# Three modulation vectors of the first layer on TensorE in column tiles instead of on VectorE

## The chip, the cores and the metric

The kernel runs on one core of one Trainium2 chip. A core has a matrix engine (TensorE, "PE" in the profile, with its weight loads as "PEld"), a vector engine (VectorE, "DVE"), a scalar engine (ScalarE, "ACT"), GpSimd ("POOL") and SyncE ("SP"), which here issues the transfers from memory. Each engine works through its own list of instructions in order and waits on semaphores for the others. The metric is the device time of one execution in microseconds (us), lower is better. The kernel before takes 1732.04 us (median of 3 runs, 1729.26 to 1732.41).

## The reference

A two-layer backbone over 512 latent tokens and 256 context tokens, width 1024, in float32. Each layer first computes six modulation vectors for the latent stream (from `c`) and six for the context (from `c_ctx`):

```python
mod   = (jax.nn.silu(c)     @ w_mod[l] + b_mod[l]).reshape(b_, 6, 1, d)
mod_c = (jax.nn.silu(c_ctx) @ w_mod[l] + b_mod[l]).reshape(6, d)
sh1, sc1, g1, sh2, sc2, g2 = [mod[:, i] for i in range(6)]
z = modulate(x, norm1_g, sh1, sc1) @ w_in          # modulate: rms_norm(x) * (1 + scale) + shift
...                                                # gMLP (A), neighbourhood attention (B), mLSTM (C)
x = x + g1 * (concat([y_a, y_b, y_c]) @ w_out)
x = x + g2 * swiglu(modulate(x, norm2_g, sh2, sc2), w_gate, w_up, w_down)
```

The change concerns vectors 2, 3 and 4 of layer 0: `g1` (the mixing gate), `sh2` and `sc2` (shift and scale of the second norm), for both streams. Each is a product of a 1024-vector with a 1024 x 1024 matrix, so 3 x 4 MB of weights for two vectors each. They are first needed after the mixing sub-layer, when the output projection's result is added to `x`.

## The kernel before

Activations are kept transposed: 128 features on the partitions, tokens along the free axis. Every float32 weight block (128 x 1024, 512 KB) is loaded into a buffer of the pool `wraw` (three buffers), split into a rounded high part `whi` on ScalarE (L128) and a rest `wlo` on VectorE (L129), each in a pool of three, and multiplied as high x high, high x low and low x high (`dense`, L152, results in `dps`). One block gives 24 products for the latents (512 columns) and 24 for the context (256 columns).

The first layer runs as follows. Vectors 0 and 1 are computed on TensorE at the start (`mod_first`, L180 to L195): the two silu'd condition vectors stand in `c_act`, padded with zeros to 32 columns for each of 8 feature blocks; a product with `c_act` as the stationary operand therefore uses a 128 x 32 column tile of the array, and four feature blocks go to the four column tiles. The 32-row partial results in PSUM (`modps`) are copied to `modsb` by ScalarE and summed over the four tiles by a small product with a selection matrix `csum` (L188).

Then comes the mixing stage, about 60 to 410 us. `ORDERS[0]` is a string that interleaves pieces of work: `B0` to `B2` attention over pairs of heads, `C0` to `C2` mLSTM, `A`, `v`, `r`, `o`, and `m`, one step of the modulation. A scheduler of the framework then sets the order of each engine's list from that program; the list is what runs. In `B`, one attention unit (`attend`) is: scores on TensorE (`bsps`, L539), bias, maximum, exponential and normalising on VectorE and ScalarE (L559 to L566, `prob`), transposition on TensorE (`ptps`, L569), copy on ScalarE (L571), product with the values (`bops`, L539). Each head pair has six units in layer 0 (three inner, one edge, two context) and four in layer 1, which has no context output.

A modulation step before (`mod_steps`, L206 to L221) is one of 24 for vectors 2, 3 and 4: a load of a 512 KB block `wmod` into a `wraw` buffer (L209), and two VectorE instructions over 128 x 1024 elements that multiply with a condition row and accumulate (L212, one for each stream). After eight steps a bias add (L217). The same function serves vector 5 and all of layer 1, later, beside the feed-forward part; that is not changed.

The output projection (`lagged`) follows at about 407 us, uses `g1` in `resid` (L1076), and its context products use the PSUM pool `md`, which has one bank.

Of the kernel before, what the change touches and what calls it, by code (L numbers as in the profile page):

```python
# [9 lines left out]
F32 = mybir.dt.float32  # L10
F32R = mybir.dt.float32r
AF = mybir.ActivationFunctionType
ALU = mybir.AluOpType
# [4 lines left out]
D = 1024  # L18
KD = 8
# [24 lines left out]
def tile_backbone(ctx: ExitStack, tc: tile.TileContext, A, out):  # L44
    nc = tc.nc
    te, ve, ac, gp, sp = nc.tensor, nc.vector, nc.scalar, nc.gpsimd, nc.sync

    const = ctx.enter_context(tc.tile_pool(name="const", bufs=1))
    par = ctx.enter_context(tc.tile_pool(name="par", bufs=1))
    hyp = ctx.enter_context(tc.tile_pool(name="hy", bufs=1))  # L50
    wraw = ctx.enter_context(tc.tile_pool(name="wraw", bufs=3))
# [15 lines left out]
    csum = cst[:, C_SUM:C_SUM + 2]  # L67
# [36 lines left out]
    def zat(name, dt=F32):  # L104
        return za.tile([128, 768], dt, tag="z", name=name)
# [97 lines left out]
    def mod_steps(l, vs):  # L203
# [20 lines left out]

        return [lambda v=v, i=i: step(v, i) for v, i in items]

    def load_small(l):
        t = par.tile([128, NSMALL], F32, tag="small%d" % l, name="small")
        link(sp.dma_start(out=t, in_=A["small"][l]))
        o, v = 0, {}  # L230
        for n, w in (("bmod", 48), ("n1", 8), ("n2", 8), ("cw", 18), ("cb", 6), ("gb", 24), ("fg", 8)):
            v[n] = t[:, o:o + w]
            o += w
        return v
# [66 lines left out]
    def x_tiles():  # L301
        return [(zat if k < 7 else zct)("x%d" % k) for k in range(KD)]

    c_act = zat("c_act")[:, 0:KD * 32].rearrange("p (k s) -> p k s", k=KD)
    gp.memset(c_act, 0.0)
    xd = drp.tile([KD, 128, 768], F32, name="xd")

# [6 lines left out]
    for toks in ((2, 3, 4, 5), (0, 1)):  # L314
        raws = []
# [127 lines left out]
    for l in range(2):  # L443
# [6 lines left out]
        latc = [P_lat] if last else [P_lat, P_ctx]  # L450
        lat_off = [(256, NL)] if last else [(256, NL), (0, NC)]
        fill_rate[0] = FILL_MIX
        mixmods = [] if last else mod_steps(0, (2, 3, 4))

        def do_mods():
            for f in mixmods:
# [768 lines left out]
def layout(inputs):  # L1225
# [14 lines left out]
    def blocks(w):  # L1240
        return w.reshape(L, w.shape[1] // 128, 128, w.shape[2] // 128, 128).transpose(0, 3, 2, 1, 4).reshape(
            L, w.shape[2] // 128, 128, w.shape[1])

    def ksplit(w, nk):
# [2 lines left out]

    wi, wg, wu, wd = I["w_in"], I["w_gate"], I["w_up"], I["w_down"]
    wm = I["w_mod"].reshape(L, D, 6, 8, 128).transpose(0, 2, 3, 4, 1)
    wm0 = I["w_mod"][0].reshape(8, 128, 6, 8, 128)[:, :, 0:2].transpose(3, 1, 0, 2, 4).reshape(8, 128, 2048)  # L1250
    arr = {
        "x": I["x"][0], "ctx": I["ctx"][0], "cond": cond, "cond_rows": np.broadcast_to(np.stack([I["c"][0], I["c_ctx"]]), (128, 2, D)), "w_mod": wm, "w_mod0": wm0, "win_blk": blocks(wi[:, :, 0:3200]),
        "win_wave": ksplit(np.concatenate([wi[:, :, 896:1024], wi[:, :, 1280:1408], wi[:, :, 512:640]], axis=2), 2),
        "win_cv": ksplit(np.concatenate([wi[:, :, 2432:2816], wi[:, :, 3200:3224]], axis=2), 2),
        "win_av": ksplit(wi[:, :, 256:512], 4), "w_out": blocks(I["w_out"]), "w_gate": blocks(wg), "w_up": blocks(wu),
# [23 lines left out]
```

## Time and profile before

| what | value |
|---|---|
| median of 3 runs | 1732.04 us |
| the profiled execution: its own time | 1729.28 us |
| its span in the profile, mean granted TensorE clock | 1726.4 us, 0.984 |
| ScalarE busy, GpSimd busy (share of the span) | 615.3 us (36%), 148.2 us (9%) |
| data moved | 184.11 MB, mean 107 GB/s |
| mixing stage of layer 0 | about 60 to 410 us |
| same stage of layer 1 | about 1050 to 1310 us |

The difference of 2.9 us between the profiled execution's time and its span lies around the traced instructions. In a group's row stand: line, engine, operation, written tile <- read tiles, shape, count | busy us, mean ns of one | idle time of the engine just before these instructions and what ended it. A product of two float32 operands has two records in the trace, so eight such products show as x16. In a row of windows stand, behind the stretch and its length, the busy us of each engine with the number of records, the granted clock, and the transfers' share and rate.

### The profile page before, as it was taken

To read this page: it belongs to the slowest core of one execution; us is meant where nothing else is said; L and a number is where in the kernel's file an instruction comes from. 1 tells how busy PE (TensorE), PEld (TensorE's weight loads), DVE (VectorE), ACT (ScalarE), POOL (GpSimd) and SP (SyncE) were. 2 spreads that over 40 slices of the span, in tenths; PEclk is the share of its full clock that TensorE was granted. 3 is DMA by queue.
4 is the path that set the end of the run, shared out by engine and by line. 5 is a ranking of instruction groups with operands and counts; after the bars stand their busy time and mean duration, and the time that the engine had idled before them with its cause. 6 is when DMAs were issued, how large, how long until landed. Compare 5 with 4: busy or idle time off the path is not lost.

```text
span 1726.4 us, 26247 instructions
## 1 busy us (share of the span) xinstructions
PE 1660.5 (96%) x10784; PEld 1416.0 (82%) x10784; DVE 936.3 (54%) x1697; ACT 615.3 (36%) x1126; POOL 148.2 (9%) x157
## 2 busy tenths in 40 slices
PE   7998999889999999999999999989989999999998
PEld 5886777768888888888888889777869988888888
DVE  4589787635475555344443355585675633333335
ACT  4444344633332211222112244534654522222225
POOL 0000112122200000000000020012033000000000
PEclk9999999979999999999999999989999999999999
DMA  8742313213244434334333233210213322222222
GB/s 290 250 151 70 123 59 102 74 35 102 62 136 132 123 122 135 125 126 128 122 122 104 74 117 105 71 56 28 86 62 117 105 98 98 93 94 94 98 82 95
DMA packets 57143, 184.11 MB, mean 107 GB/s; under 512 B 6720, under 2 KB 8384, under 8 KB 56896
## 3 DMA queue, kind: packets, MB, share of 16 engines
q1 hardware_dynamic: 57024, 182.45, 32.7%
q8 instruction: 84, 1.38, 0.3%
q14 instruction: 35, 0.29, 0.1%
HBM read 175.08 MB, written 7.34 MB: 106 GB/s over the span
## 4 chain that ended last, share of the span: by engine, by line
PE 69%; DVE 5%; ACT 2%; POOL 1%; issue 1%; DVEq 0%; ACTq 0%; POOLq 0%
PE dps L152 60%; PE wps L402 4%; PE vps L627 2%; PE ptps L569 1%; PE nps L876 1%; DVE wlo L129 1%; PE bops L539 1%; ACT pu L862 1%; DVE nm L561 0%; ACT prob L564 0%; DVE prob L566 0%; ACT whi L128 0%; PE bsps L539 0%; DVE bsps L559 0%; PE ups L832 0%
## 5 line engine op out<-in xcount | busy, mean ns | idle before, releaser
L128 ACT ACTIVATE whi<-wraw 128x1024 fp32r<-128x1024 f32 (+2 forms) x224 | 226.6, 1013 | 694.8 <-PE dps L152 429.7
L129 DVE TENSOR_TENSOR wlo<-wraw,whi 128x1024 fp32r<-128x1024 f32 (+2 forms) x224 | 262.5, 1173 | 170.7 <-ACT whi L128 167.9
L152 PE MATMUL dps<-h2lh,wlo 128*128 128x512 f32 (+1 forms) x664 | 258.3, 391 | 0.0
L152 PE MATMUL dps<-h2ll,whi 128*128 128x512 f32 (+1 forms) x664 | 258.3, 391 | 0.0
L152 PE MATMUL dps<-h2lh,whi 128*128 128x512 f32 (+1 forms) x664 | 257.6, 389 | 0.0
L152 PE MATMUL dps<-gh,whi 128*128 128x512 f32 (+1 forms) x576 | 175.2, 341 | 0.0
L152 PE MATMUL dps<-gl,whi 128*128 128x512 f32 (+1 forms) x576 | 175.2, 340 | 0.0
L152 PE MATMUL dps<-gh,wlo 128*128 128x512 f32 (+1 forms) x576 | 175.1, 340 | 0.0
L212 DVE SCALAR_TENSOR_TENSOR wmod<-wmod,c_all 128x1024 f32<-128x1024 f32 x80 | 98.5, 1231 | 98.5 <-DMA wmod<-in_w_mod 97.7
L152 PEld LDWEIGHTS dps<-h2lh,whi 128*128 128x128 f32 x664 | 124.3, 188 | 27.7
L152 PEld LDWEIGHTS dps<-h2lh,wlo 128*128 128x128 f32 x664 | 124.2, 188 | 27.4
L152 PEld LDWEIGHTS dps<-h2ll,whi 128*128 128x128 f32 x664 | 124.3, 188 | 26.7
L1076 DVE SCALAR_TENSOR_TENSOR x<-dps,modT,x 128x512 f32<-128x512 f32 (+1 forms) x112 | 65.3, 596 | 138.0 <-PE dps L152 137.7
L152 PE MATMUL dps<-ll,whi 128*128 128x512 f32 x336 | 136.6, 407 | 1.2 <-DVE ll L109 1.2
L152 PE MATMUL dps<-lh,whi 128*128 128x512 f32 x336 | 134.8, 402 | 1.1 <-ACT whi L128 1.1
L152 PE MATMUL dps<-lh,wlo 128*128 128x512 f32 x336 | 134.7, 401 | 0.0
L152 PEld LDWEIGHTS dps<-gl,whi 128*128 128x128 f32 x576 | 99.3, 188 | 13.5 <-DVE gl L109 0.2
L152 PEld LDWEIGHTS dps<-gh,whi 128*128 128x128 f32 x576 | 99.3, 188 | 13.2
L152 PEld LDWEIGHTS dps<-gh,wlo 128*128 128x128 f32 x576 | 99.3, 188 | 13.2
L212 DVE SCALAR_TENSOR_TENSOR junk<-wmod,c_all 128x1024 f32<-128x1024 f32 x48 | 58.9, 1227 | 76.8 <-DMA wmod<-in_w_mod 76.8
L1153 DVE TENSOR_TENSOR silu<-silu,dps 128x512 f32<-128x512 f32 (+1 forms) x64 | 37.4, 589 | 107.4 <-PE dps L152 107.4
L152 PE MATMUL dps<-h2cl,whi 128*128 128x256 f32 x328 | 92.5, 282 | 0.0
(320 smaller groups left out, 3123.2 us busy)
## 6 DMA issues: line engine op xcount, KB each, us to landing
wmod<-in_w_mod SPq DMA_DIRECT2D x80, 512.0 KB, 3.6
wraw<-in_w_up SPq DMA_DIRECT2D x42, 512.0 KB, 3.2
wraw<-in_w_gate SPq DMA_DIRECT2D x40, 512.0 KB, 3.2
wraw<-in_win_blk SPq DMA_DIRECT2D x34, 512.0 KB, 3.7
wraw<-in_w_down SPq DMA_DIRECT2D x32, 512.0 KB, 3.2
wraw<-in_w_out SPq DMA_DIRECT2D x19, 512.0 KB, 3.3
wraw<-in_w_down SPq DMA_DIRECT2D x21, 384.0 KB, 3.1
wraw<-in_win_cv SPq DMA_DIRECT2D x16, 408.0 KB, 3.2
```

The source lines that it names most:

```text
L128: ac.activation(out=hi[:, 0:n], in_=raw[:, 0:n], func=AF.Copy)
L129: ve.tensor_tensor(out=lo[:, 0:n], in0=raw[:, 0:n], in1=hi[:, 0:n].bitcast(F32), op=ALU.subtract)
L152: m = te.matmul(out=ps[:, 0:T], lhsT=wt[:, c], rhs=(flo if wh else fhi)(k), start=(k == 0 and wi == 0), stop=(k == nk - 1 and wi == 2),)
L212: ve.scalar_tensor_tensor(out=junk if t < nt - 1 else raw, in0=raw, scalar=1.0, in1=c_all[:, t, :], op0=ALU.mult, op1=ALU.mult, accum_out= ...
L402: m = te.matmul(out=ps[:, 0:T], lhsT=wt[:, cs_], rhs=(flo if wh else fhi)(k), start=(k == 0 and wi == 0), stop=(k == KD - 1 and wi == 2))
L539: m = te.matmul(*args, **kw)
L569: te.transpose(out=tps[:, i * 128:(i + 1) * 128], in_=pt[:, i * 128:(i + 1) * 128], identity=ident)
L627: te.matmul(out=vps[i][:, 0:408], lhsT=tokslice(nm, k, i), rhs=wt[:, cs], start=(k == 0 and wi == 0), stop=(k == KD - 1 and wi == 2))
L862: tabled.append(ac.activation(out=tc_, in_=pc, func=AF.Exp, scale=-1.0, bias=g_))
L876: m = te.matmul(out=banks[j][64 * hf:64 * hf + 64, c * 65:(c + 1) * 65], lhsT=lhsT, rhs=rhs, start=start, stop=stop, skip_group_check=True)
L1076: ve.scalar_tensor_tensor(out=xs, in0=ps, scalar=modT[:, row * 8 + k, g[3]:g[3] + 1], in1=xs, op0=ALU.mult, op1=ALU.add)
L1153: ve.tensor_tensor(out=s, in0=s, in1=pui, op=ALU.mult)
```

## The change

`mod_steps(0, (2, 3, 4))` in the mixing stage is replaced by `mod_pe_steps()`. There are again 24 steps, one for a vector v and a block i of 128 outputs. Step n loads the block of step n + 1 (the first step loads its own too) into a `wraw` buffer and multiplies the block it holds with `c_act`: eight products of 128 columns into one of the four quarters of a PSUM bank of the pool `md`. After every fourth step ScalarE copies the bank to `modsb` (128 x 512), four small products with `csum` sum the column tiles, and VectorE adds the bias for four blocks at once. So `c_act` has to live on: it moves from a `za` buffer to the constants. The weights come in another layout (`w_modp`), with the same bytes. `ORDERS` is the same.

```diff
+    def mod_pe_steps():
+        modT, sm = mods[0], smalls[0]
+        items = [(v, i) for v in (2, 3, 4) for i in range(KD)]
+        raws, bank = {}, [None]
+
+        def load(n):
+            if n < len(items):
+                v, i = items[n]
+                raws[n] = wraw.tile([128, D], F32, tag="w", name="wmod")
+                sp.dma_start(out=raws[n], in_=A["w_modp"][v - 2, i])
+
+        def step(n):
+            v, i = items[n]
+            if n == 0:
+                load(0)
+            load(n + 1)
+            raw = raws.pop(n)
+            q = i % 4
+            if q == 0:
+                bank[0] = pst(md, "modps")
+            ps = bank[0]
+            for kp in range(KD):
+                te.matmul(
+                    out=ps[32 * (kp % 4):32 * (kp % 4) + 32, q * 128:(q + 1) * 128], lhsT=c_act[:, kp, :],
+                    rhs=raw[:, kp * 128:(kp + 1) * 128], start=(kp < 4), stop=(kp >= 4), tile_position=(0, 32 * (kp % 4)))
+            if q < 3:
+                return
+            sb = wkt("modsb")
+            ac.activation(out=sb, in_=ps, func=AF.Copy)
+            for c in range(4):
+                te.matmul(out=ps[:, 2 * c:2 * c + 2], lhsT=sb[:, c * 128:(c + 1) * 128], rhs=csum)
+            r = v * 8 + i - 3
+            ve.tensor_tensor(
+                out=modT[:, r:r + 4, :], in0=ps[:, 0:8].rearrange("p (c t) -> p c t", c=4),
+                in1=sm["bmod"][:, r:r + 4].unsqueeze(2).to_broadcast([128, 4, 2]), op=ALU.add)
+            if v == 4 and i == KD - 1:
+                ve.scalar_tensor_tensor(
+                    out=a2s[0], in0=modT[:, 32:40, :], scalar=1.0, in1=sm["n2"].unsqueeze(2).to_broadcast([128, 8, 2]),
+                    op0=ALU.add, op1=ALU.mult)
+
+        return [lambda n=n: step(n) for n in range(len(items))]
...
-    c_act = zat("c_act")[:, 0:KD * 32].rearrange("p (k s) -> p k s", k=KD)
+    c_act = const.tile([128, KD * 32], F32, name="c_act").rearrange("p (k s) -> p k s", k=KD)
...
-        mixmods = [] if last else mod_steps(0, (2, 3, 4))
+        mixmods = [] if last else mod_pe_steps()
...
+    wmp = I["w_mod"][0].reshape(8, 128, 6, 8, 128)[:, :, 2:5].transpose(2, 3, 1, 0, 4).reshape(3, 8, 128, 1024)
```

Lines behind the new function stand 42 further on in the changed kernel: `ptps` is L569 before and L611 after, `bops` and `bsps` L539 and L581. The new products are L249, the small ones L257, the new loads L236.

The change moves instructions on all engines of the mixing stage. Three places matter. First SyncE's list, where the weights of `B1` (`win_blk`, the first three of them) stand among the loads of the modulation; the number behind a name tells one buffer's use from the next, and in brackets are the semaphores waited for. Before:

```order
L209 DMA wmod_1432<-in_w_mod 128x1024 [waits DMAHW4_49,DVE_49]
L209 DMA wmod_1561<-in_w_mod 128x1024 [waits DMAHW0_49,DVE_49]
L125 DMA wraw_1568<-in_win_blk 128x1024 [waits DMAHW1_49,DVE_49]
L125 DMA wraw_1628<-in_win_blk 128x1024 [waits DVE_49]
L125 DMA wraw_1688<-in_win_blk 128x1024 [waits DMAHW3_49,DVE_49]
```

Now:

```order
L236 DMA wmod_1424<-in_w_modp 128x1024 [waits DMAHW3_49,PE_49]
L236 DMA wmod_1453<-in_w_modp 128x1024 [waits DMAHW4_49,DMAHW0_49,PE_49]
L236 DMA wmod_1595<-in_w_modp 128x1024 [waits DMAHW6_49,DMAHW1_49,PE_49]
L125 DMA wraw_1609<-in_win_blk 128x1024 [waits DMAHW7_49,PE_49]
L569 DMA bias_1800<-in_bias 128x384 [waits DVE_49]
L569 DMA bias_1802<-in_bias 128x384 [waits DVE_49]
L125 DMA wraw_1669<-in_win_blk 128x1024 [waits DMAHW2_49,DVE_49,Activation_49]
```

The loads of the modulation, and the first weight load behind them, now wait for TensorE (`PE_49`), which has to have used the block that a buffer held; before they waited for VectorE alone.

Second, TensorE's list at the third inner unit of `B0`, from the transposition of its probabilities to the first dense products behind the edge unit's scores. Before:

```order
L569 MATMUL ptps<-cst,prob 128x128 x4
L152 MATMUL dps<-lh,wlo 128x512
L152 MATMUL dps<-ch,wlo 128x256
L152 MATMUL dps<-lh,whi 128x512
L152 MATMUL dps<-ch,whi 128x256
L539 MATMUL bops<-probT,bvt 64x128 x8
L539 MATMUL bsps<-bk,bq 64x128 x4
L539 MATMUL bsps<-bk,bq 128x256 x2
L152 MATMUL dps<-ll,whi 128x512
```

Now:

```order
L249 MATMUL modps<-wmod,c_act 32x128
L611 MATMUL ptps<-cst,prob 128x128 x4
L249 MATMUL modps<-wmod,c_act 32x128 x23
L611 MATMUL ptps<-cst,prob 128x128 x4
L581 MATMUL bops<-probT,bvt 64x128 x8
L581 MATMUL bsps<-bk,bq 64x128 x4
L581 MATMUL bsps<-bk,bq 128x256 x2
L152 MATMUL dps<-lh,whi 128x512
L152 MATMUL dps<-ch,whi 128x256
```

Three steps' products (24) stand in one bunch where dense products stood, and the dense products behind are the first of `B1`, with the weights `wraw_1609` of the list above, whose load waits for the last of these 24.

Third, TensorE's list at the first inner unit of `B1`, behind its scores `bsps`. Before:

```order
L478 MATMUL trps<-cst,bv 128x128 x4
L152 MATMUL dps<-lh,wlo 128x512
L539 MATMUL bsps<-bk,bq 128x256 x4
L152 MATMUL dps<-ch,whi 128x256
L152 MATMUL dps<-cl,whi 128x256
L152 MATMUL dps<-ch,wlo 128x256
```

Now:

```order
L520 MATMUL trps<-cst,bv 128x128 x6
L581 MATMUL bsps<-bk,bq 128x256 x4
L249 MATMUL modps<-wmod,c_act 32x128 x24
L611 MATMUL ptps<-cst,prob 128x128 x8
L152 MATMUL dps<-lh,whi 128x512
L152 MATMUL dps<-ch,whi 128x256
```

Before, 30 dense products stood between the scores and the first transposition; now it is 24 products of the modulation alone, and the dense products behind the transpositions start a new block, whose load waits for the middle eight of the 24.

More of the change, by code (lines that the diff above doesn't have):

```diff
@@ L1249, in layout @@
     wm = I["w_mod"].reshape(L, D, 6, 8, 128).transpose(0, 2, 3, 4, 1)
+    wmp = I["w_mod"][0].reshape(8, 128, 6, 8, 128)[:, :, 2:5].transpose(2, 3, 1, 0, 4).reshape(3, 8, 128, 1024)
     wm0 = I["w_mod"][0].reshape(8, 128, 6, 8, 128)[:, :, 0:2].transpose(3, 1, 0, 2, 4).reshape(8, 128, 2048)
     arr = {
-        "x": I["x"][0], "ctx": I["ctx"][0], "cond": cond, "cond_rows": np.broadcast_to(np.stack([I["c"][0], I["c_ctx"]]), (128, 2, D)), "w_mod": wm, "w_mod0": wm0, "win_blk": blocks(wi[:, :, 0:3200]),
+        "x": I["x"][0], "ctx": I["ctx"][0], "cond": cond, "cond_rows": np.broadcast_to(np.stack([I["c"][0], I["c_ctx"]]), (128, 2, D)), "w_mod": wm, "w_mod0": wm0, "w_modp": wmp, "win_blk": blocks(wi[:, :, 0:3200]),
         "win_wave": ksplit(np.concatenate([wi[:, :, 896:1024], wi[:, :, 1280:1408], wi[:, :, 512:640]], axis=2), 2),
```

## The prediction

> **What bounds the kernel now.** I read the page's busy times first, then the chain of work that ended last.
>
> ```profile
> span 1726.4 us, 26247 instructions
> PE 1660.5 (96%) x10784; PEld 1416.0 (82%) x10784; DVE 936.3 (54%) x1697; ACT 615.3 (36%) x1126; POOL 148.2 (9%) x157
> PE 69%; DVE 5%; ACT 2%; POOL 1%; issue 1%; DVEq 0%; ACTq 0%; POOLq 0%
> ```
>
> TensorE is busy for 96% of the span and carries 69% of the chain. Work added to it costs its own length unless it falls into an idle gap; work taken from VectorE gains only where TensorE waits for VectorE. So the question is how much TensorE idles, and for whom, in the stage that loses the VectorE work. The windows compare that stage with the same stage of layer 1, which has the same attention code and no modulation on VectorE:
>
> ```profile
> core 0: us, PE busy (x) PEld busy (x) DVE busy (x) ACT busy (x) POOL busy (x), PEclk, DMA share, GB/s
> 60.00:410.00 350.00, 316.76 (x2594) 263.12 (x2593) 253.39 (x542) 161.94 (x354) 54.89 (x54) 0.96 0.31 101
> 1050.00:1310.00 260.00, 243.34 (x1976) 201.67 (x1975) 165.77 (x366) 127.66 (x267) 46.45 (x52) 0.97 0.21 66
> ```
>
> In 60 to 410 us TensorE idles 350 - 316.8 = 33.2 us, and the clock that it is granted is 0.96, which is another 14 us of full speed. No gain in this stage can be above 47 us. In layer 1, idle is still 16.7 us of 260. The waits of TensorE, in 60 to 410 us (first three rows) and in 1050 to 1310 us (last row):
>
> ```profile
> PE ptps L569 <- DVE prob L566: 18.0, 12, 4.9
> PE sps L803 <- DVE rden L902: 2.1, 1, 2.1
> PE trps L478 <- DVE ck L772: 1.4, 1, 1.4
> ...
> PE ptps L569 <- DVE prob L566: 6.1, 10, 1.4
> ```
>
> More than half of the idle time is the softmax: the transposition waits until VectorE has normalised the probabilities.
>
> **What is removed.** The instructions at L212 in that stage, one row for each stream:
>
> ```profile
> L212 DVE SCALAR_TENSOR_TENSOR junk<-wmod,c_all x24: 1204/1222/1455, 84.1 to 309.6; 128x1024 f32<-128x1024 f32 x24
> L212 DVE SCALAR_TENSOR_TENSOR wmod<-wmod,c_all x24: 1202/1220/1896, 85.4 to 311.9; 128x1024 f32<-128x1024 f32 x24
> ```
>
> 48 instructions of 1.22 us are 58.6 us of VectorE's 253.4. VectorE is not the bound, so this is not a gain by itself. Where an L212 stands between two steps of a softmax, it delays `prob` by 1.2 us. Layer 1 shows what is left without them: 6.1 us in 12 attention units (three head pairs, four units each). Layer 0 has 18 units, so 6.1 x 18 / 12 = 9.2 us would stay, and 18.0 - 9.2 = 8.8 us go. Of the other two waits, 3.5 us, I take 2.2. **Term 1: -11 us.** Bounds: 0, since the new order also puts less work under some softmaxes (below), and -21.5, all three waits gone.
>
> **The clock.** The loss is concentrated late in the stage:
>
> ```profile
> 250.00:290.00 40.00, 33.49 (x270) 27.08 (x269) 32.85 (x64) 12.77 (x33) 11.58 (x14) 0.91 0.17 54
> 330.00:370.00 40.00, 30.35 (x305) 24.09 (x305) 16.30 (x42) 15.07 (x35) 8.38 (x6) 0.79 0.12 36
> 353.15 0.66 PE L569 MATMUL ptps<-cst,prob 128*128 128x128 f32 x2 [2.32 <-DVE prob L566]
> ```
>
> 330 to 370 us alone loses 0.21 x 40 = 8.4 us, in a stretch where TensorE idles 9.7 us in gaps of at most 2.3. In the new list this stretch (the end of `B2`) has 37 dense products under the edge unit and 25 of the modulation under the last context unit, so most of its gaps should go. **Term 2: -7 us**, half of the 14. Bounds: -14, and +5 if the new gaps below slow the clock elsewhere by about half as much as 330 to 370 us does now. The Trainium skill, TensorE: Matmul & The Clock Gate, section "Why this matters for your kernels", asks for no idle gap above about 3 us, since an idle window of that length halves the clock. The trace shows a lower clock with no gap above 2.3 us in that stretch, so it does not bear the rule out as a limit on single gaps; by the rule there would be nothing to win here and the sum would come out 7 us higher.
>
> **What is added: the column-tile products.** Start-up does the same product with 256 columns. Timeline of TensorE there:
>
> ```profile
> 44.52 0.28 PE L402 MATMUL wps<-cl,whi 128*128 128x256 f32 x1
> 44.64 0.39 PE L402 MATMUL wps<-lh,wlo 128*128 128x512 f32 x1
> 44.87 0.28 PE L402 MATMUL wps<-ch,wlo 128*128 128x256 f32 x1
> 45.08 1.07 PE L180 MATMUL modps<-wmod,c_act 128*32 128x256 f32 x16
> 46.08 0.39 PE L402 MATMUL wps<-ch,whi 128*128 128x256 f32 x1
> 46.89 0.50 PE L188 MATMUL modps<-cst,modsb 128*128 128x2 f32 x4
> 47.25 0.49 PE L402 MATMUL wps<-lh,whi 128*128 128x512 f32 x1
> L180 PEld LDWEIGHTS modps<-wmod,c_act x48: 106/110/110, 45.1 to 55.2; 128*32 128x32 f32 x48
> L180 PE MATMUL modps<-wmod,c_act x48: 379/379/403, 45.1 to 55.4; 128*32 128x256 f32 x48
> ```
>
> Starts tell the cost, since records overlap: a dense product costs 0.23 us with 512 columns (44.64 to 44.87) and 0.12 with 256. The eight column-tile products cost 46.08 - 44.87 - 0.12 = 1.09 us. Their 16 records of 0.379 us make 6.1 us within 1.07, so four tiles do run side by side, in four rounds. With 128 columns the cost is between half, 0.55, and the same, 1.09. I take 0.70: four rounds, each no shorter than a weight load of 0.11, are 0.44, and filling and emptying the array, about a quarter of a microsecond, does not shrink with the columns. **Term 3: 24 x 0.70 = +16.8 us**, bounds 13.2 and 26.2. Four records of L188 cost 47.25 - 46.89 = 0.36 us; each of the six groups has eight, 0.72. **Term 4: +4.3 us**, bounds 2.2 (no more than four cost now) and 6 (each a stop of its own of 1 us, as the wait for `modsb` may add). The six copies to `modsb` and six bias adds lie on engines that are idle half the time; uncovered they would be six times about 0.6 us, which the upper bound of term 4 holds.
>
> **What is moved: the weight loads.** A `wraw` buffer is now released by TensorE's own list. At the five places where a bunch of modulation products is followed by a new dense block, the block's load starts when the bunch is nearly through. What the load and the split take, and what TensorE has meanwhile:
>
> ```profile
> wraw<-in_win_blk SPq DMA_DIRECT2D x17, 512.0 KB, 3.7
> L128 ACT ACTIVATE whi<-wraw 128x1024 fp32r<-128x1024 f32 x171 | 181.4, 1061 | 621.2 <-PE dps L152 405.8 <-issue 198.1 <-PE vps L627 7.5
> L129 DVE TENSOR_TENSOR wlo<-wraw,whi 128x1024 fp32r<-128x1024 f32 x171 | 211.0, 1235 | 135.2 <-ACT whi L128 132.4 <-PE dps L152 0.3
> 129.36 0.60 PE L569 MATMUL ptps<-cst,prob 128*128 128x128 f32 x4
> 130.65 1.09 PE L539 MATMUL bops<-probT,bvt 128*64 128x128 f32 x16
> 131.67 1.08 PE L539 MATMUL bsps<-bk,bq 64*64 64x128 f32 x12
> L571 ACT ACTIVATE probT<-ptps 128x512 f32<-128x512 f32 x36 | 21.4, 594 | 36.5 <-PE ptps L569 36.4
> ```
>
> The first dense product can start 3.7 + 1.06 = 4.8 us after the release. At `B0`'s edge unit TensorE has 0.60 (`ptps`), 0.59 waiting for `probT`, 1.02 (`bops`) and 1.08 (`bsps`), 3.3 in all: 1.5 us late, and `wlo`, 1.24 later, has only 0.70 of dense work ahead of it: 0.5 more. At `B1`'s first unit it has the last eight modulation products (0.7), 1.2 of transpositions and a wait of about half a microsecond: 2.4 late. The other three, counted likewise from the new list, come to 2.0, 0.7 and 1.1. Everything on TensorE queues behind these dense products, the next `ptps` included. **Term 5: +9 us**, more exactly 2.0 + 2.4 + 2.0 + 0.7 + 1.1 = 8.2, and nearly one more for ScalarE's and VectorE's lists, where the split stands behind softmax steps. Bounds: 0, if these waits only replace softmax waits, and 20, if each place loses 4 us. In the trace before, TensorE hardly ever waits for `whi` in this stage, since VectorE frees the buffers early. The need for cover is read in layer 1's chain:
>
> ```profile
> 1095.80 1.11 PE bsps L539 x8
> 1096.91 0.74 DVE bsps L559 x2
> 1098.37 0.79 ACT prob L564 x2
> 1100.01 0.63 PE ptps L569 x4
> ```
>
> From scores to transposition 1100.01 - 1096.91 = 3.1 us pass. 24 modulation products, 3 x 0.70 = 2.1 us, do not cover that, where 30 dense ones (15 x 0.35 = 5.3) did; so part of the softmax wait stays, as term 1 has it. The other moves cost nothing: the bytes loaded are the same, `c_act` in the constants frees a buffer, and the last step ends before the second norm needs it, behind 50 us of output projection; without that cover it would cost its own 0.7 + 0.7 us.
>
> **The sum.** -11 - 7 + 16.8 + 4.3 + 9 = +12.1 us. The profiled execution took 1729.28 us (span 1726.4 and 2.9 around it), which gives 1741.4; it stands 2.8 us under the median of the runs, so against the median it would be 1744. I take **1742 us**, 0.6% slower.
>
> **The rivals.** *Relief wins (faster).* If softmax waits shrink to almost nothing, the clock stays up and the loads are not late, the sum is -21.5 - 14 + 13.2 + 4.3 = -18 us, 1711; a milder case, -16 - 10 + 14 + 4 + 2 = -6, gives 1723 on the profiled time and 1726 on the median. For it speaks that more than half of the stage's idle time waits for VectorE, and that the new products can stand in gaps; against it, that layer 1 keeps 16.7 us of idle time with VectorE free. It decides once waits and clock give back more than 21 us. *Even.* Terms 1 and 2 at -18 against 3 to 5 at +20: within 0.2% (3.5 us, about what a measurement can tell from no change), some 1732. *The buffers starve TensorE (much slower).* Three `wraw` buffers serve both streams of loads, and two of them hold blocks for later steps for long stretches; if each of the five places loses 4 us (20), half of term 1 goes and the clock falls (+5), it is -5.5 + 5 + 16.8 + 4.3 + 20 = +41 us, 1770. It decides when the loads land later than 3.7 us or the splits queue for over 2 us. *No side-by-side tiles.* At 16 records one after another, 0.11 each, a step costs 1.8 us, 42 in all in place of 16.8, +37 us, 1767; the start-up rows show four at once, so 2%.
>
> **Chances.** Forecast, 3.5 to 30 us slower: 0.52. Starving or no tiling, more than that: 0.08. Even: 0.16. Faster: 0.24. So faster 0.24, same 0.16, slower 0.60. The range of 8 in 10 reaches into the faster case, to 1724, and up to 1762; the forecast's own is 1735 to 1759.
>
> **What would show it.** In the new profile: L249 with 24 bunches at 0.6 to 0.8 us from start to next start; `ptps` waiting for `prob` about 9 us in the stage; new waits of dense products for `whi` and `wlo` of 6 to 10 us, the first behind `B0`'s edge scores; clock in the stage near 0.98; the stage's end, the start of the output projection, moved from 407 to about 419 us and nothing changed behind it. Waits for `prob` of 3 us with no waits for `whi` would make it wrong, as would bunches at over 1 us.

## The result and the profile after

The changed kernel takes 1753.8 us (median of 4 runs, 1752.3 to 1754.8) against 1730.7 us of the kernel before (4 runs beside them, 1727.0 to 1732.4). The ratio is 1.0145, 95% interval [1.0129, 1.016]: 23 us slower, where 11 to 12 had been forecast. The sign and the range held; the size is about twice the forecast's. The two profiled executions are 1754.8 and 1729.3 us, 25.5 apart, so sizes read from this pair of traces run about 2 us high.

The head of the new page, its busy times, and the chain's shares by engine:

```profile
span 1753.2 us, 27015 instructions
PE 1687.4 (96%) x11216; PEld 1434.5 (82%) x11216; DVE 886.7 (51%) x1604; ACT 619.0 (35%) x1132; POOL 148.5 (8%) x157
PE 78%; DVE 7%; ACT 3%; issue 1%; POOL 1%; DMA 1%; DVEq 0%; ACTq 0%; POOLq 0%; SPq 0%
```

VectorE is busy for 49.6 us less (the 48 removed instructions add up to 58.6, but records on VectorE overlap); TensorE is busy for 26.9 us more. All of the loss lies in the first layer's attention stage. The chain of waits of the kernel before, where the output projection starts and the dense run behind it (the view's window cuts the last piece short, so only its start counts):

```profile
407.45 51.77 PE dps L152 x288
...
493.36 6.71 PE dps L152 x38
```

and of the changed kernel:

```profile
434.46 52.10 PE dps L152 x297
...
520.68 39.45 PE dps L152 x223
```

The projection starts 27.0 us later, and from there to the start of the last piece shown the two run alike (85.9 and 86.2 us). The span grew by 26.8. The stage from 60 us to that point, by windows, first before and then after:

```profile
60.00:407.45 347.45, 314.21 (x2580) 260.93 (x2579) 250.84 (x536) 160.13 (x351) 54.89 (x54) 0.96 0.31 101
```

```profile
60.00:434.46 374.46, 341.23 (x2988) 278.71 (x2987) 200.21 (x439) 161.13 (x356) 55.10 (x54) 0.94 0.29 93
```

Columns are as in the prediction: length, TensorE, its weight loads, VectorE, ScalarE, GpSimd, then the granted clock. TensorE idles 347.45 - 314.21 = 33.2 us before and 374.46 - 341.23 = 33.2 us after. With 50 us less work on VectorE, not one microsecond of idle time is gone, and the clock fell from 0.96 to 0.94. In these traces the clock is either full or half, the half in pieces of 3.4 us or several in a row (before, 158.6 to 162.0 us is at 0.50, with 1.00 on both sides). Each can cost up to 1.7 us; this stage has 9 such pieces before and 14 after, at most 15.4 and 23.9 us. So the stage got longer by TensorE's added work and by clock, and the idle time in sum shows no relief.

Whom TensorE waits for in that stage now:

```profile
PE ptps L611 <- DVE prob L608: 14.3, 11, 5.0
PE sps L845 <- DVE cq L814: 4.3, 2, 3.2
PE dps L152 <- ACT whi L128: 4.2, 3, 1.9
PE bops L581 <- ACT probT L613: 2.2, 2, 1.8
PE dps L152 <- DVE wlo L129: 1.3, 1, 1.3
```

The softmax wait went from 18.0 to 14.3, not to 9. Direct waits for late weights, `whi` and `wlo`, are 5.5 us. The first of them stands where the prediction put it, behind the scores of `B0`'s edge unit (timeline, in square brackets the idle time before and its releaser):

```profile
115.11 0.41 PE L249 MATMUL modps<-wmod,c_act 128*32 128x128 f32 x2
115.54 0.63 PE L611 MATMUL ptps<-cst,prob 128*128 128x128 f32 x4
116.10 1.51 PE L249 MATMUL modps<-wmod,c_act 128*32 128x128 f32 x46
118.71 0.63 PE L611 MATMUL ptps<-cst,prob 128*128 128x128 f32 x4 [1.10 <-DVE fa L691]
121.12 1.98 PE L581 MATMUL bops<-probT,bvt 128*64 128x128 f32 x16 [1.78 <-ACT probT L613]
123.02 1.86 PE L581 MATMUL bsps<-bk,bq 64*64 64x128 f32 x12
126.16 0.80 PE L152 MATMUL dps<-lh,whi 128*128 128x512 f32 x1 [1.27 <-ACT whi L128]
...
129.12 0.79 PE L152 MATMUL dps<-lh,wlo 128*128 128x512 f32 x1 [1.31 <-DVE wlo L129]
```

Between 115.1 and 126.2 us no dense product runs, since the next block's weights are not there. Four gaps of 1.1 to 1.8 us follow; the last two are waits for weights, the first two are waits for VectorE and ScalarE that have no dense products under them. Even the records are longer from 121 us on (the 16 of `bops` take 1.98 us, 1.09 in the prediction's rows): the clock has halved. Windows on three such places:

```profile
121.00:134.00 13.00, 10.30 (x49) 7.73 (x50) 6.60 (x16) 5.06 (x10) 1.70 (x1) 0.50 0.40 127
185.00:196.00 11.00, 7.16 (x67) 5.32 (x59) 5.43 (x10) 4.65 (x8) 0.00 (x0) 0.69 0.62 194
280.00:291.00 11.00, 9.75 (x70) 6.71 (x70) 5.39 (x12) 4.88 (x14) 4.55 (x6) 0.56 0.21 82
```

The chain of waits shows the late blocks more plainly than the rows of waits do. Where TensorE waits for `whi` for the third time:

```profile
231.44 4.36 DMA wraw<-in_win_blk
235.82 1.06 ACT whi L128
236.93 4.36 PE dps L152 x14
```

A transfer into `wraw` stands in this chain, which reaches back to 148 us, four times (231, 291, 298 and 418 us), 16.1 us in all. In the chain of the kernel with one buffer for the blocks alone (next section), which reaches back to 60 us, there is none.

The place that the prediction had singled out is the end of `B2`. The last four attention units normalise their probabilities between 329.3 and 363.9 us before and between 344.9 and 385.6 us in the changed kernel, so these stretches are compared, first before and then after:

```profile
329.30:363.90 34.60, 24.85 (x224) 19.20 (x225) 13.63 (x36) 12.49 (x30) 6.55 (x4) 0.75 0.10 31
344.90:385.60 40.70, 36.38 (x395) 30.24 (x395) 19.94 (x46) 25.12 (x46) 9.34 (x6) 0.92 0.20 58
```

It recovered in good part: 9.8 us idle became 4.3, and 0.75 became 0.92. Similar losses came up elsewhere, at the three places above.

The products themselves cost no more than was forecast: counted as in the prediction a bunch of eight costs 0.67 us (0.58 from its start to the next start), and one of 24 takes 1.5 us, under three times 0.70. So a bunch covers little of a softmax, and many in one cover less than their count.

### The profile page after: what moved, and what is told of

Same layout as the page of the kernel before. It is cut to its first block, busy times and chain, and to the rows that moved or that the text cites. A ratio compares the mean times of both kernels' runs of the same rounds, so it can differ in the third digit from the quotient of the medians.

```text
span 1753.2 us, 27015 instructions
## 1 busy us (share of the span) xinstructions
PE 1687.4 (96%) x11216; PEld 1434.5 (82%) x11216; DVE 886.7 (51%) x1604; ACT 619.0 (35%) x1132; POOL 148.5 (8%) x157
## 4 chain that ended last, share of the span: by engine, by line
PE 78%; DVE 7%; ACT 3%; issue 1%; POOL 1%; DMA 1%; DVEq 0%; ACTq 0%; POOLq 0%; SPq 0%
PE dps L152 64%; PE wps L444 3%; PE vps L669 2%; PE ptps L611 1%; PE bops L581 1%; PE bsps L581 1%; PE nps L918 1%; DVE wlo L129 1%; DVE prob L608 1%; ACT prob L606 1%; PE avps L984 1%; DMA wraw<-in_win_blk 1%; PE modps L249 1%; DVE rM L737 1%; ACT whi L128 1%
## 5 line engine op out<-in xcount | busy, mean ns | idle before, releaser
L212 DVE SCALAR_TENSOR_TENSOR wmod<-wmod,c_all 128x1024 f32<-128x1024 f32 x56 | 68.6, 1224 | 98.8 <-DMA wmod<-in_w_mod 98.2
L152 PE MATMUL dps<-h2ch,wlo 128*128 128x256 f32 x328 | 92.0, 281 | 0.0
L152 PE MATMUL dps<-h2ch,whi 128*128 128x256 f32 x328 | 91.7, 280 | 0.0
```

The lines of the kernel that those rows point to most:

```text
L152: m = te.matmul(out=ps[:, 0:T], lhsT=wt[:, c], rhs=(flo if wh else fhi)(k), start=(k == 0 and wi == 0), stop=(k == nk - 1 and wi == 2),)
L212: ve.scalar_tensor_tensor(out=junk if t < nt - 1 else raw, in0=raw, scalar=1.0, in1=c_all[:, t, :], op0=ALU.mult, op1=ALU.mult, accum_out= ...
```

## The experiments

All times are medians; each difference is of medians, against runs of the kernel before on the same chip (1727 to 1729 us). The ratio with its 95% interval is estimated from all runs, and can differ a little from that of the medians. The theory, A: the blocks of the modulation take weight buffers that TensorE gives back late, so dense weights come late, and with them goes the cover of the softmaxes and the clock. Its rival, B: the price is the added TensorE work itself, and 32-column products do not hold the clock.

**The relief alone.** Two kernels before the change without VectorE's work; both leave the three vectors uncomputed. In the first the loads stay, and one tiny copy frees each buffer:

```diff
-            for t in range(nt):
+            if l == 0 and v in (2, 3, 4):
+                ve.tensor_copy(out=modT[:, v * 8 + i, 0:nt], in_=raw[:, 0:nt])
+            for t in range(0 if l == 0 and v in (2, 3, 4) else nt):
```

> The kernel before, with the two long VectorE instructions of each of the 24 steps replaced by one short copy of two columns (the three vectors are then not computed); the loads and their buffers stay, released by VectorE. It prices the relief of VectorE alone, without any work on TensorE. My terms 1 and 2 expect -11 - 7 = -18 us against the kernel before, waits of ptps for prob near 9 us and the clock in the stage at 0.98. Rival (the order of TensorE's list sets the waits, not VectorE's load): no more than -6 us, waits for prob still 14 us or more.

In the second the 24 steps are gone, loads and all:

```diff
-        mixmods = [] if last else mod_steps(0, (2, 3, 4))
+        mixmods = []
+        if not last:
+            ve.memset(modT[:, 16:40, :], 0.5)
+            ve.memset(a2s[0], 1.0)
```

> The kernel before without the 24 steps: no loads, no VectorE work, no TensorE work for the three vectors (constants stand in their place, so they are not computed). It is the floor of any way to compute them. If the relief of VectorE is worth -18 us, this run is at -18 or a little better, since the wraw buffers are free too. By the rival it is near -6 us. The changed kernel then costs the difference to +23 over that floor.

Measured: 1716.8 us, -10.9 (ratio 0.9942 [0.9925, 0.996]), and 1715.3 us, -12.4 (0.9928 [0.9912, 0.9945]). Relief is real, and to have none of this work in the stage is worth about 12 us, not 18. The stage of the second:

```profile
60.00:394.95 334.95, 310.80 (x2568) 258.11 (x2567) 199.23 (x433) 159.83 (x352) 54.15 (x54) 0.96 0.20 66
```

Idle is 24.2 us (33.2 before), and the clock stays at 0.96 (8 half pieces in the place of 9). TensorE's waits for `prob` are 8.9 us there, which is what the prediction had worked out from layer 1. In the first kernel they are still 14.5, in a trace of the slowest of its runs. So in this trace a free VectorE gives back idle time and hardly any clock. Over whole executions some clock came back too: its mean is 0.987 to 0.988 in the four runs of the second kernel and 0.984 on average before, by an estimate from these 6 us at most.

**The blocks in a buffer of their own.** The changed kernel, with blocks in the scratch tile `junk`, which nothing uses in this stage; the call that loads the next block moves behind the eight products, so it starts when TensorE has used the last one. The three `wraw` buffers serve weights alone.

```diff
-                raws[n] = wraw.tile([128, D], F32, tag="w", name="wmod")
+                raws[n] = junk
...
-            load(n + 1)
             raw = raws.pop(n)
...
+            load(n + 1)
```

> The changed kernel, but the blocks of the modulation are loaded into one buffer of their own (a scratch tile that is idle in this stage), the next one as soon as TensorE has used the last; the weights keep all three wraw buffers. TensorE's products stay 24 x 8. Theory A (shared buffers: steps come in bunches, weights arrive late, softmaxes stand uncovered, the clock falls): gives back 10 us or more of the 23, waits for whi gone, clock of the stage back to 0.96 or more. Theory B (the price is the TensorE work itself, and a clock that column tiles do not hold): gives back 5 us or less, clock still near 0.94.

Measured: 1729.8 us, +2.0 (1.0015 [1.0006, 1.0025]). 21 of the 23 us are gone, with the same 192 products and 24 loads. Its stage:

```profile
60.00:406.97 346.97, 329.20 (x3013) 269.66 (x3013) 205.18 (x445) 162.59 (x358) 53.42 (x54) 1.00 0.31 100
```

Idle is 17.8 us and the clock 1.00. B falls: column-tile products do not lower the clock, and their work is not what costs the 21 us. At the place shown above, dense products stand again between the steps of the softmax, and the eight products fill a gap between them (timeline):

```profile
118.73 0.28 PE L152 MATMUL dps<-ch,wlo 128*128 128x256 f32 x1
118.94 0.64 PE L248 MATMUL modps<-junk,c_act 128*32 128x128 f32 x16
119.52 0.50 PE L152 MATMUL dps<-lh,whi 128*128 128x512 f32 x1
...
120.43 0.63 PE L611 MATMUL ptps<-cst,prob 128*128 128x128 f32 x4
120.82 0.48 PE L152 MATMUL dps<-lh,whi 128*128 128x512 f32 x1
```

**Is it the bunches or the buffers?** With one own buffer the bunches of 24 are gone too. So two own buffers in turn (`junk` and half of `c_all`, whose own load moves to a later place), with one step loaded ahead again, which puts some bunches in pairs (the edit is shown against the kernel with one own buffer, without the moved load):

```diff
-                raws[n] = junk
+                raws[n] = junk if n % 2 else c_all[:, 0, :]
...
+            load(n + 1)
...
-            load(n + 1)
```

> The changed kernel with the modulation's blocks in two buffers of their own in turn (the idle junk tile and half of c_all, which is loaded later for its own use), so a block is loaded one step ahead again, but no weight load waits for it. All is computed. In the list of TensorE the bunches of eight then stand in pairs in about half of the places, as in the changed kernel, while the weights' three buffers stay the weights' own. Beside the kernel with one buffer (+2 us against the kernel before): if the bunching is what costs (uncovered softmaxes, a falling clock), 8 to 15 us slower than before and the half clock is back; if it is the weights' buffers that cost, within 4 us of the kernel with one buffer, that is 0 to +6 us.

Measured: 1730.0 us, +2.2 (1.002 [1.0005, 1.0036]). Pairs of bunches cost nothing that can be measured. Three in a row did not occur here; the kernel with four shared buffers and no load ahead, below, has them.

**How many buffers?** The changed kernel without the step loaded ahead; with four shared buffers instead of three; and with both.

```diff
-            if n == 0:
-                load(0)
-            load(n + 1)
+            load(n)
```

> The changed kernel, each step loading its own block instead of the next step's, so that no block waits in a wraw buffer for a later step. Theory A: fewer buffers are held, so bunches and late weights shrink, 4 to 10 us better than the changed kernel unless TensorE now waits for the blocks themselves. Theory B: within 3 us of the changed kernel.

```diff
-    wraw = ctx.enter_context(tc.tile_pool(name="wraw", bufs=3))
+    wraw = ctx.enter_context(tc.tile_pool(name="wraw", bufs=4))
-    junk = const.tile([128, D], F32, name="junk")
+    junk = const.tile([128, D], mybir.dt.bfloat16, name="junk")
```

> The changed kernel with four weight buffers instead of three, shared as before by weights and modulation blocks, and with the block of the next step loaded ahead; the scratch output of the other modulation instructions, which nobody reads, is stored in half the bytes to make room. All is computed. If what costs is that too few buffers are left for weights while one or two hold blocks for later steps, one more buffer gives most of it back: 0 to 8 us slower than the kernel before. If sharing itself costs (a released buffer goes to whichever load was issued first, and TensorE releases late), 15 us or more stay.

> The changed kernel with four shared buffers and without the load ahead, so that at most one buffer holds a modulation block that is in use, as in the kernel with one buffer of its own (+2 us). All is computed. If the number of buffers left for weights is what counts, 0 to 5 us slower than the kernel before. If sharing itself costs, because buffers are handed out in turn and a weight block must wait for the modulation block whose place it gets, 9 us or more slower, not far below the 15 of four shared buffers with the load ahead.

Measured: 1745.3 us, +17.6 (1.0104 [1.0089, 1.0119]); 1744.0 us, +15.2 (1.0088 [1.0071, 1.0106]); 1729.6 us, +2.4 by the medians (1.0006 [0.9995, 1.0018]). Put in a table by what is left for weights when blocks hold as many buffers as the code lets them:

| kernel | buffers | held by blocks | left for weights | against before |
|---|---|---|---|---|
| changed | 3 shared | 2 | 1 | +23.2 us |
| no load ahead | 3 shared | 1 | 2 | +17.6 |
| four shared | 4 shared | 2 | 2 | +15.2 |
| four shared, no load ahead | 4 shared | 1 | 3 | +2.4 |
| one of its own | 3 + 1 | 1 of its own | 3 | +2.0 |
| two of its own | 3 + 2 | 2 of its own | 3 | +2.2 |

The price goes by the number left for weights, and with three left it makes no difference whether the buffers are shared. The third row missed its expectation of 0 to 8 us and came out where the rival had it, that handing out in turn costs by itself; the fourth row, at +2.4 where that rival asked for 9 or more, refutes it. The kernel of the fourth row also has two bunches of 24 products and one of 21 (179, 261 and 360 us in its trace), so it is not the bunches. One thing stays open: fewer buffers change both the order that the scheduler writes and the moment at which a block lands, and no run holds the order fixed. The waits of four shared buffers, in 60 to 407 us:

```profile
PE ptps L611 <- DVE prob L608: 9.6, 11, 2.2
PE dps L152 <- ACT whi L128: 4.8, 3, 3.7
PE sps L845 <- DVE cq L814: 3.7, 2, 2.8
```

and of the same without the load ahead:

```profile
PE ptps L609 <- DVE prob L606: 9.4, 14, 1.9
PE sps L843 <- DVE cq L812: 3.1, 2, 2.0
PE dps L152 <- ACT bk L553: 3.0, 1, 3.0
PE dps L152 <- ACT whi L128: 2.3, 2, 1.7
```

These differ by 13 us in time and by 2.5 us in waits for `whi`. Their stages tell more, first the four shared, then those without the load ahead:

```profile
60.00:422.68 362.68, 334.45 (x3000) 274.43 (x2999) 200.07 (x441) 162.38 (x357) 55.70 (x54) 0.96 0.30 97
```

```profile
60.00:408.93 348.93, 326.71 (x2990) 268.02 (x2990) 198.22 (x440) 162.21 (x357) 53.95 (x54) 0.98 0.31 100
```

28.2 against 22.2 us idle, and 0.96 against 0.98 clock (8 and 4 half pieces). The rows of waits name who came last at each gap; they do not show what a late block took away from under other gaps, nor the clock.

**Does sharing cost while VectorE uses the blocks?** The kernel before, with one own buffer for the 24 blocks. (Here, and in the kernels below with a tile `own`, the scratch output `junk`, which nobody reads, takes half the bytes to make room.)

```diff
-            raw = wraw.tile([128, D], F32, tag="w", name="wmod")
+            raw = own if l == 0 and v in (2, 3, 4) else wraw.tile([128, D], F32, tag="w", name="wmod")
```

> The kernel before, all 24 steps on VectorE in the attention stage, with one buffer of their own (and the scratch output, which nobody reads, stored in half the bytes to make room). All is computed. If sharing costs whenever it is there, this is 5 us or more faster than the kernel before; if it costs only where TensorE releases the blocks late, it is within 3 us of it.

Measured: 1731.8 us, +4.7 by the medians (1.0025 [1.0012, 1.0038]). No gain, and a loss a little beyond the 3 us that had been allowed for: where VectorE is the user, sharing three buffers costs nothing that an own buffer would give back. (Its profiled execution took 9 us more than the median, so its trace is not read here.)

**What the products themselves cost.** The kernel with one own buffer, with half of the products (it leaves out half of each sum):

```diff
-            for kp in range(KD):
+            for kp in range(4):
...
-                    rhs=raw[:, kp * 128:(kp + 1) * 128], start=(kp < 4), stop=(kp >= 4), tile_position=(0, 32 * (kp % 4)))
+                    rhs=raw[:, kp * 128:(kp + 1) * 128], start=True, stop=True, tile_position=(0, 32 * (kp % 4)))
```

> The one-buffer kernel with only the first four of the eight products of each step (the other half of the sum over the input channels is left out, so three modulation vectors are wrong by that half); loads, copies, closing products and the order around them stay. It prices terms 3 and 4. By the forecast a bunch of four is two rounds of 0.11 plus a fixed quarter of a microsecond, 0.45 to 0.5 instead of 0.70, so 24 steps give back about 5 us: 3 us faster than before. If the bunches' time was mostly inside gaps that TensorE has anyway, it gives back under 2 us; if a step costs by its records, it gives back 8 us or more.

Measured: 1724.9 us, -2.9 (0.9974 [0.996, 0.9989]), that is 4.9 us under the kernel with all of them. The forecast's size lies there: four of a bunch's eight products are two rounds of 0.11 us, 24 times 0.22 are 5.3. But the ten runs spread from 1718.9 to 1727.3 us, and by the means the difference is 7 us, so this supports the size without fixing it.

**Where does the relief sit, and can it be had?** The next kernels keep steps on VectorE but move them behind the start of the output projection, where VectorE is less than half busy (25.2 of 60 us in 400 to 460 us before). The first two only issue them there:

```diff
-        mixmods = [] if last else mod_steps(0, (2, 3, 4))
+        mixmods = [] if last else mod_steps(0, (2, 3))
...
+        if not last:
+            fill.extend(mod_steps(0, (4,)))
+        fill_rate[0] = 1
         preload(AF.Sqrt, tabled)
```

> The kernel before, VectorE method for all three vectors, but the eight steps of the last vector (the second norm's scale) are issued in the output projection, one behind each dense block, instead of in the attention stage. All is computed. If VectorE's load near the softmaxes is what costs there, a third of the 11 to 12 us that leaving out all 48 instructions gave comes back, more since the late part of the stage had the lowest clock: 4 to 7 us faster, the output projection's 52 us unchanged, as VectorE has 17 of 50 us there and gets 19.6 more. If the loads or VectorE's splits delay the projection's blocks, the gain is lost: within 2 us.

> As the one before, but with sixteen steps, both vectors of the second norm, in the output projection, two behind each dense block. All is computed. By the relief: two thirds of 11 to 12 us, 8 us faster, if the projection hides 39 us more of VectorE on top of 17 in 52. If VectorE is full there, the splits of the projection's blocks come late and the second norm waits for its vectors: 0 to 10 us slower than before.

Measured: 1726.7 us, -1.0 (0.9998 [0.9987, 1.001]) and 1731.6 us, +3.8 (1.0021 [1.001, 1.0032]). They do not test what they were made for, since the scheduler put the late steps back into the stage, all of them in the first kernel and most in the second (groups of L212 from 320 us on in the first, with first and last start):

```profile
L212 DVE SCALAR_TENSOR_TENSOR junk<-wmod,c_all x8: 1215/1223/1645, 326.1 to 381.8; 128x1024 f32<-128x1024 f32 x8
```

So the next two hold each late step behind a dense block of the projection, by an order dependence on the load and on its first instruction. A third does it with the mixing gate on TensorE, through one own buffer.

```diff
-            sp.dma_start(out=raw, in_=A["w_mod"][l, v, i])
+            d_ = sp.dma_start(out=raw, in_=A["w_mod"][l, v, i])
+            if l == 0 and v in LATE:
+                pe_ = last_pe[0]
+                after(d_, pe_)
...
+                if l == 0 and v in LATE and t == 0:
+                    after(i_, pe_)
```

> The kernel before with the eight steps of the second norm's scale on VectorE in the output projection, and now held there by an order (each step's load and first instruction are placed behind a dense block of the projection), since without it the scheduler put them back to 326 to 398 us. All is computed. By the relief, a third of the 11 to 12 us: 3 to 5 us faster. If the relief came mostly from the early steps, or the projection's blocks suffer, within 2 us.

> The same with sixteen steps, both vectors of the second norm, held in the output projection, two behind each dense block. All is computed. By the relief 6 to 9 us faster, if VectorE's 39 us more fit into the projection's 52 us beside its 17; if they don't, weights of the projection come late and the second norm starts late: 2 us faster to 10 us slower.

> The one-buffer kernel with only the mixing gate (eight steps) as column-tile products on TensorE, and the second norm's shift and scale on VectorE, held in the output projection. All is computed. No modulation instruction is left on VectorE in the attention stage. By the sum: 12 us of relief, eight steps at 14.5 / 24 = 0.6 us give 4.8 back: 7 us faster. If the output projection doesn't hold the sixteen steps, the kernel with sixteen late steps shows the same loss, and this one stands 3 to 5 us below it.

Measured: 1762.7 us, +33.9 (1.0203 [1.0186, 1.022]); 1777.7 us, +48.9 (1.0288 [1.0271, 1.0305]); 1784.9 us, +56.2 (1.0328 [1.0312, 1.0345]). All far off what was expected, and all in the projection. Chain of waits of the first there:

```profile
400.89 6.02 DMA wmod<-in_w_mod
406.93 1.24 DVE junk L216 x2
408.20 1.23 DVE wmod L216 x2
409.43 1.16 DVE junk L216 x2
410.65 1.11 issue
411.85 1.15 DVE wlo L130
413.04 10.47 PE dps L153 x44
```

Weights, modulation and dense blocks run in turn instead of side by side. Is VectorE too full, or are the weights starved? The same eight steps with a buffer of their own, and an order for the load alone:

```diff
-            raw = wraw.tile([128, D], F32, tag="w", name="wmod")
-            sp.dma_start(out=raw, in_=A["w_mod"][l, v, i])
+            late = l == 0 and v == 4
+            raw = own if late else wraw.tile([128, D], F32, tag="w", name="wmod")
+            ld = sp.dma_start(out=raw, in_=A["w_mod"][l, v, i])
+            if late:
+                after(ld, last_pe[0])
```

> The eight late steps on VectorE in the output projection, held behind its dense blocks, but with a buffer of their own instead of the weights' buffers, where the shared one lost 34 us. All is computed. If those 34 us were starved weights, the stage's 9 us come through: 6 to 9 us faster than the kernel before, less up to 3 us if the eighth step, some 50 us after the first, is late for the second norm. If VectorE was too full for the projection's splits, 10 us slower or more.

Measured: 1722.3 us, -4.9 (0.9971 [0.9955, 0.9987]). 39 us lie between two kernels that do the same work in the same place. TensorE's waits from 396 to 470 us, all of them:

```profile
PE msps L264 <- DVE sqacc L257: 2.7, 1, 2.7
PE wps L406 <- DVE h2ll L292: 0.8, 1, 0.8
```

No wait for weights is left, so VectorE was not too full. Two things differ between the two, the buffer and the order on the first instruction; the two were not tried apart. The 3.5 us that are left fall where the last late steps still run on VectorE, up to 454 us, beside the start of the second norm. With two of the eight steps back in the stage:

> As the kernel with eight late steps in a buffer of their own, but with two of the eight back in the attention stage, so six are late and end some 12 us before the second norm needs them. All is computed. If the 4 us lost there are the late end, these come back and the stage gives up a quarter of its 9 us: 6 to 8 us faster than the kernel before. If the relief hangs on the very last steps, or the projection's splits queue behind the late steps, no better than 5 us.

Measured: 1721.5 us, -6.3 (0.9963 [0.995, 0.9976]): faster than the kernel before and the changed one, though against the eight late steps 0.8 us is within the noise. Neither of the two waits is left between 396 and 470 us. Its projection starts at 399.3 us and is as long as before:

```profile
399.31 51.76 PE dps L152 x288
```

Last, the change itself for the last eight steps alone, through an own buffer, with the first sixteen on VectorE as before:

> Sixteen steps (mixing gate, second norm's shift) on VectorE as before, through the shared buffers, and the last eight (its scale) as column-tile products on TensorE with a buffer of their own. All is computed. If the relief sits in the late part of the stage, 9 us are gained and eight steps at 0.6 us give 4.8 back: 4 us faster than the kernel before. If the relief is spread over the steps, a third of 12 less 4.8: no difference, within 2 us.

Measured: 1723.8 us, -3.4 by the medians (0.9976 [0.9962, 0.9991]). Six late steps taken out of the stage gain 6.3 us, all 24 some 11 to 12: about half of the relief hangs on the last quarter of the steps, which ran at 267 to 313 us before. For these last steps even the column-tile products pay.

## Why the prediction was right or wrong

Four kernels split the result: from the kernel before to the one without steps -12.4, from there to the one with an own buffer +14.5, from there to the changed kernel +21.1; together +23.2. Against the terms, this is -18 forecast for 1 and 2, +21.1 for 3 and 4, +9 for 5.

- **Term 5, the late weight loads, is the step that failed.** It was +9 with a bound of 20, and it measured 21. The mechanism was right, and so was the first place: a buffer comes free late by TensorE's own list, the first block late is the one behind `B0`'s edge scores. At the second place, `B1`'s first unit, no product waits for `whi`: the two transpositions ahead of it wait 1.67 and 2.17 us for `prob` (187.5 and 190.3 us), and the block is there by then. It was priced as the direct wait for `whi` and `wlo` at five places, and these waits are 5.5 us, under the forecast. What was left out is that a late block is also the cover of the softmax around it, and that with the cover goes the clock: own buffer against changed kernel, idle is 17.8 against 33.2 us and the clock 1.00 against 0.94 (0.988 to 0.992 against 0.981 to 0.983 over whole executions, some 15 us). The terms were added as if each stood alone. Term 5 takes terms 1 and 2 away. How the 21 us split between lost cover and clock is read from one trace each, and no run separates them.
- **Terms 1 and 2, -11 and -7.** Together they were too large even for a VectorE without the work, -10.9 to -12.4. Term 1 was nearly right there: the waits for `prob` fell to 8.9 us and the idle time by 9.1. Of the clock's 7 little came (0.96 stays in the stage; 6 us at most over whole executions). In the changed kernel neither is seen: the idle time is the same, which is term 1's bound of 0, and the clock's half pieces add up to 8.5 us more in this pair of traces, past term 2's bound of +5. Over whole executions the mean clock, 0.982 against 0.984, makes it 3 to 4, so the sign was wrong and the bound stays open.
- **Terms 3 and 4, +16.8 and +4.3.** The sizes hold roughly: 0.67 us for a bunch of eight, less for each of three in a row, and 5 to 7 us for half of the products where the same formula gives 5.3. Net, with a buffer of their own, they cost +14.5: some of the products fill gaps (idle 17.8 us, 24.2 without steps), and the clock is higher with them (1.00 against 0.96).
- **The signals.** Bunches at 0.6 to 0.8 us from start to start: 0.58 for one of eight, just under; several steps ran as one bunch. Waits for `prob` of about 9: no, 14.3. Waits for `whi` and `wlo` of 6 to 10: 5.5. Clock near 0.98: no, 0.94. The projection's start at about 419: 434.5. Nothing changed behind it: yes.
- **The rivals.** "The buffers starve TensorE" had the mechanism, with half of term 1 lost and the clock down, at +41 us, in a chance of 0.08 that it shared with another. It deserved more: it is what happened, at a little over half its price, with waits of 5.5 us instead of 20 and with all of term 1 lost instead of half. "Relief wins" needed terms 1 and 2 above 21 us, and without the work the kernel gains 12. Tiles run side by side, so the last rival fell.
- **The sum and the range.** The forecast was +11 to +12 against +23.2. With an own buffer the same terms without the fifth are -11 - 7 + 16.8 + 4.3 = +3.1, and +2.0 was measured there: right, though partly by luck, since an excess of 6 in the first two stands against one of 7 in the next two.

## What to carry to other kernels

When work moves to another engine, ask who frees its buffers from then on: a pool shared with the stream that feeds the bound engine is priced by how many buffers stay for that stream (here three: +2 us, two: +15 to +18, one: +23), not by the waits that name it. A late weight block costs its own wait, and beside that the cover that it was for other waits, and the clock; in this stage the second part, by subtraction, was nearly three times the first. Relief of an engine that is not the bound need not be spread evenly: here six of 24 steps moved to the projection, with a buffer of their own, gave 6 of 12 us.

## What was not expected of the hardware

The clock halved with no single gap above 1.8 us: 0.50 in 121 to 134 us. Ahead of it stand gaps of 1.10 and 1.78 us with only 0.63 us of work between them (from 117.61 to 121.12 us by the rows above), and within it gaps of 1.27 and 1.31. The kernel with one own buffer has a wait for `prob` of 5.7 us in 140 to 180 us and loses less there (all waits of this kind in the stage, and the window):

```profile
PE ptps L611 <- DVE prob L608: 11.8, 12, 5.7
```

```profile
140.00:180.00 40.00, 32.90 (x253) 25.58 (x253) 29.66 (x75) 18.35 (x48) 5.91 (x11) 0.96 0.13 39
```

0.04 of 40 us are 1.6 us, one half piece of the clock, where the stretch with the short gaps lost 0.50 of 13, that is 6.5. The Trainium skill, TensorE: Matmul & The Clock Gate, section "Why this matters for your kernels", warns of single idle gaps above about 3 us. The gap of 5.7 us agrees, as a half piece goes with it; the stretch at 0.50 does not. Little work for TensorE over the 3.5 us ahead, rather than the length of one gap, looks like the better warning; no run varied that alone, so it stays open.

Column-tile products do not by themselves lower the clock (1.00 with all 192 of them), and they get cheaper in bunches: eight take 0.64 us, 23 in a row 1.51 (the 46 records at 116.10 us), which by estimate is a fixed 0.2 and 0.11 for every two products.
